# Two waits of a VectorE sum change places: the load on the sum, the earlier sum in a nop in front

## The chip, the cores and the metric

One core of a Trainium2 chip runs the kernel. The metric is device time in microseconds (us) of one execution; "the span" is the profiled execution from its first to its last instruction, 1.78 us shorter (160.52 of 162.30 us before).

## The reference

```python
x = random (32, 512, 1024) float32;  multiplier = 0.5
return (np.sum(x, axis=-1) * multiplier).astype(np.float32)
```

16,384 row sums over 67.11 MB of input; the output is 64 KB.

## The kernel before

Each of 128 partitions holds 128 rows, loaded 16 at a time. VectorE sums most blocks with one reduction. The last block comes in pieces, and its last row in two, cut at column 576, so that little work is left once the last bytes have landed.

```python
def nop_after(engine, waits_for, follows):
    i = engine.nop()
    for w in waits_for:
        tc.add_manual_dep(i.ins, w.ins.name, SYNC, reason="end seen here")
    for f in follows:
        tc.add_manual_dep(i.ins, f.ins.name, ORDER, reason="in this order")
    return i

def dve_span(t, r, lo, hi, dst, start=0.0):
    mid = (lo + hi) // 2
    return nc.vector.tensor_tensor_reduce(     # adds the two halves, then all of it to start
        out=t[:, r, lo:mid], in0=t[:, r, lo:mid], in1=t[:, r, mid:hi],
        scale=mul, scalar=start, op0=ADD, op1=ADD, accum_out=dst)
# ... all blocks but the last ...
cut = 576
# ... loads of rows 0-7, 8-12, 13-14 of the last block ...
for lo, hi in ((0, cut), (cut, D)):
    loads.append(nc.sync.dma_start(out=t[:, B - 1, lo:hi], in_=x_last[:, B - 1, lo:hi]))
# ... the other rows of the block, on VectorE and ScalarE ...
dve_span(t, B - 1, 0, cut, part)
final = dve_span(t, B - 1, cut, D, res[:, rows - 1 : rows], start=part)
# ... SyncE waits for everything and stores the last 16 columns ...
```

## Time and profile before

| | before |
|---|---|
| time, median of 3 | 162.13 us (162.12 to 162.49) |
| span | 160.5 us |
| last load lands | 157.72 us |
| last sum starts | 157.85 us |
| from the last landing to the end of the span | 2.80 us |

The table is read from the bottom. Up to 157.72 the loads run, and their queue is busy for 97.5% of the span; the last 2.80 us run one after the other: the last sum, its store, the closing barrier. Only the first 0.13 us of that, between landing and sum, is touched here.

### The profile page before, as it was taken

To read this page: it belongs to the slowest core of one execution; us is meant where nothing else is said; L and a number is where in the kernel's file an instruction comes from. 1 tells how busy PE (TensorE), PEld (TensorE's weight loads), DVE (VectorE), ACT (ScalarE), POOL (GpSimd) and SP (SyncE) were. 2 spreads that over 40 slices of the span, in tenths; PEclk is the share of its full clock that TensorE was granted. 3 is DMA by queue.
4 is the path that set the end of the run, shared out by engine and by line. 5 is a ranking of instruction groups with operands and counts; after the bars stand their busy time and mean duration, and the time that the engine had idled before them with its cause. 6 is when DMAs were issued, how large, how long until landed. Compare 5 with 4: busy or idle time off the path is not lost.

```text
span 160.5 us, 138 instructions
## 1 busy us (share of the span) xinstructions
DVE 119.3 (74%) x34; ACT 17.3 (11%) x31; POOL 0.2 (0%) x4
## 2 busy tenths in 40 slices
DVE  0000059998699968999599995999959999597443
ACT  0000000000000000000000000000000000599952
POOL 0000000000000000000000000000000000000000
DMA  8996996996996996996996997997998998999991
GB/s 261 523 523 261 523 506 278 523 490 294 523 490 294 523 490 294 523 490 294 523 490 294 523 474 310 523 441 343 523 425 359 523 425 359 392 433 425 439 368 50
DMA packets 2016, 67.18 MB, mean 418 GB/s; under 512 B 480, under 2 KB 608, under 8 KB 736
## 3 DMA queue, kind: packets, MB, share of 16 engines
q1 hardware_dynamic: 2016, 67.18, 97.5%
HBM read 67.11 MB, written 0.07 MB: 418 GB/s over the span
## 4 chain that ended last, share of the span: by engine, by line
DMA 75%; DVE 22%; SPq 1%; issue 0%; DVEq 0%
DMA xb<-in_x_dram 75%; DVE sums L96 21%; SPq L114 1%; DVE xb L80 0%; SPq L120 0%; SPq L94 0%; DVE res L99 0%; DVEq L80 0%; DVEq L201 0%
## 5 line engine op out<-in xcount | busy, mean ns | idle before, releaser
L96 DVE TENSOR_REDUCE sums<-xb 128x16 f32<-128x16384 f32 (+1 forms) x7 | 112.0, 16001 | 33.6 <-DMA xb<-in_x_dram 33.6
L70 ACT ACT_TABLE_LOAD x1 | 1.3, 1283 | 138.2 <-DMA xb<-in_x_dram 138.2
L70 ACT ACTIVATE xb<-xb 128x1024 f32<-128x1024 f32 x15 | 15.7, 1045 | 2.1 <-DMA xb<-in_x_dram 2.1
L80 DVE CUSTOM_DVE_ANT_0 xb<-xb 128x512 f32<-128x512 f32 (+1 forms) x9 | 5.6, 663 | 5.0 <-DMA xb<-in_x_dram 5.0
L70 ACT ACTIVATION_READ_ACCUMULATOR xb<-xb 128x1 f32 x15 | 2.8, 187 | 0.0
L99 DVE TENSOR_SCALAR res<-sums 128x16 f32<-128x16 f32 (+1 forms) x7 | 1.2, 174 | 0.2
L80 DVE DVE_READ_ACCUMULATOR2_ANT res<- 128x1 f32 x9 | 0.7, 83 | 0.0
L80 DVE CUSTOM_DVE_ANT_0 xb<-xb,part 128x224 f32<-128x224 f32 x1 | 0.5, 452 | 0.2 <-DMA xb<-in_x_dram 0.2
L187 POOL MEMSET const-bfloat16-1.0<- 128x1 bf16 x1 | 0.1, 102 | 0.0
L187 POOL MEMSET const-uint8-127<- 128x1 uint8 x1 | 0.1, 102 | 0.0
L187 POOL MEMSET const-float32-0.0<- 128x1 f32 x1 | 0.1, 99 | 0.2 <-issue 0.2
L187 POOL MEMSET const-float32-1.0<- 128x1 f32 x1 | 0.1, 99 | 0.0
L80 DVE DVE_READ_ACCUMULATOR2_ANT part<- 128x1 f32 x1 | 0.1, 83 | 0.0
## 6 DMA issues: line engine op xcount, KB each, us to landing
xb<-in_x_dram SPq DMA_DIRECT2D x1, 4096.0 KB, 31.1
xb<-in_x_dram SPq DMA_DIRECT2D x1, 2560.0 KB, 36.9
xb<-in_x_dram SPq DMA_DIRECT2D x1, 1024.0 KB, 38.9
xb<-in_x_dram SPq DMA_DIRECT2D x1, 288.0 KB, 39.1
xb<-in_x_dram SPq DMA_DIRECT2D x1, 224.0 KB, 39.2
xb<-in_x_dram SPq DMA_DIRECT2D x7, 40.8
out_dram<-res SPq DMA_DIRECT2D x1, 56.0 KB, 10.0
out_dram<-res SPq DMA_DIRECT2D x1, 8.0 KB, 1.4
```

Of the source, the lines that this page charges most:

```text
L70: acts.append(nc.scalar.activation(out=t[:, r, :], in_=t[:, r, :], func=mybir.ActivationFunctionType.Copy, scale=mul, accum_out=res[:, col ...
L80: return nc.vector.tensor_tensor_reduce(out=t[:, r, lo:mid], in0=t[:, r, lo:mid], in1=t[:, r, mid:hi], scale=mul, scalar=start, op0=ADD, o ...
L96: nc.vector.reduce_sum(out=sums[:, c0 : c0 + h], in_=t[:, 0:h, :], axis=mybir.AxisListType.X)
L99: nc.vector.tensor_single_scalar(out=res[:, c0 : c0 + h], in_=sums[:, c0 : c0 + h], scalar=mul, op=mybir.AluOpType.mult,)
L114: nc.sync.dma_start(out=t[:, lo:hi, :], in_=x_last[:, lo:hi, :])
L187: nc = _bacc.Bacc("TRN2", target_bir_lowering=False, num_devices=1)
```

## The change

The last sum needs two things: the last load, and part, the sum over the row's first 576 columns. The intent is to let it wait for the load alone, the later of the two, and to have the wait for part over and done with ahead of it.

```diff
-    dve_span(t, B - 1, 0, cut, part)
+    first = dve_span(t, B - 1, 0, cut, part)
+    part_seen = nop_after(nc.vector, [first], [])
     final = dve_span(t, B - 1, cut, D, res[:, rows - 1 : rows], start=part)
+
+    tc.add_manual_dep(final.ins, part_seen.ins.name, ORDER, reason="in this order")
+    tc.declare_no_dep(final.ins, first.ins.name, reason="waited for by the nop in front")
```

The diff seems to add an instruction; the prediction shows from the built programs that it does not, since an event-semaphore instruction (here one that only waits for semaphores; 21 ns on VectorE's sequencer in the trace before) already stood in front of the sum. Below, **old form** means load in front and part on the sum; **new form** means part in front and load on the sum.

## The prediction

Cut out of the recorded text below, and marked there, are a paragraph and a sentence on how the sequencer works, which no run here shows; that the wait for part has to stay somewhere was argued in them alone and is not shown either. Part's arm comes to -46 + 28 + 21 + 91 = +94 ns and the load's to 0 + 24 = +24, all from the trace before. "In that place" means the event-semaphore instruction in front of the sum, which loses the wait for the load.

> **What bounds the kernel now.** I read the page first, then the chain that ended last, then the instructions in order of time over the last microsecond, then the row view of the line that forms the sums, and last the trace's own semaphore records.
>
> The page gives the scale of things:
>
> ```profile
> span 160.5 us, 138 instructions
> DVE 119.3 (74%) x34; ACT 17.3 (11%) x31; POOL 0.2 (0%) x4
> q1 hardware_dynamic: 2016, 67.18, 97.5%
> DMA 75%; DVE 22%; SPq 1%; issue 0%; DVEq 0%
> ```
>
> The one DMA queue fills 97.5% of the 16 engines' time, and the loads carry three quarters of the chain. VectorE is busy 74% of the span and nothing near full. So the kernel is bound by reading 67.11 MB, and no arithmetic ahead of the last load can shorten it. The change touches only what follows that load. This is the end of the chain, with start, length and owner of each piece:
>
> ```profile
> 118.50 39.21 DMA xb<-in_x_dram
> 157.72 0.03 issue
> 157.74 0.02 DVEq L80
> 157.76 0.09 issue
> 157.85 0.45 DVE xb L80
> 158.31 0.01 DVEq L201
> ```
>
> The last load lands at 157.72. The last sum, which needs nothing else from memory, starts only at 157.85. Of that gap, a piece of 0.02 us is work of VectorE's sequencer (DVEq), with 0.03 before it and 0.09 after. Compare a place where the sum waits for its load itself, earlier in the same chain:
>
> ```profile
> 58.63 40.79 DMA xb<-in_x_dram
> 99.42 0.02 issue
> 99.44 17.23 DVE sums L96
> ```
>
> There the sum starts 0.02 us after the landing. So the last sum loses about 0.11 us (0.13 - 0.02) against an instruction that waits for its load itself. The row view of the summing line names the piece between, and the timeline gives the neighbours:
>
> ```profile
> L80 DVEq EVENT_SEMAPHORE  x1: 21/21/21, 157.7 to 157.7; - x1
> ```
>
> ```profile
> 157.19 0.46 DVE L80 CUSTOM_DVE_ANT_0 xb<-xb 128x288 f32<-128x288 f32 x1
> 157.41 0.19 ACT L70 ACTIVATION_READ_ACCUMULATOR xb<-xb 128x1 f32 x1
> 157.57 0.08 DVE L80 DVE_READ_ACCUMULATOR2_ANT part<- 128x1 f32 x1
> 157.85 0.45 DVE L80 CUSTOM_DVE_ANT_0 xb<-xb,part 128x224 f32<-128x224 f32 x1 [0.20 <-DMA xb<-in_x_dram]
> 158.23 0.08 DVE L80 DVE_READ_ACCUMULATOR2_ANT res<- 128x1 f32 x1
> 158.34 0.34 SPq L138 DMA_DIRECT2D out_dram<-res  x1
> ```
>
> The reader is to see that the value the last sum starts from (part) is finished at 157.57 + 0.08 = 157.65, only some 0.06 us ahead of the landing, and that the store follows the last sum directly.
>
> **What the built programs add.** The diff seems to add an instruction, but it doesn't. In the kernel before, the builder has already split the last sum's two waits: an event-semaphore instruction waits for the last load, and the sum itself waits for part. In the changed kernel the nop is that event-semaphore instruction: it waits for part, and the sum itself waits for the last load. Order, count and operands on every engine are the same, and SyncE's waits ahead of the store are unchanged. The change is a swap of two waits between two instructions.
>
> [...]
>
> **The change, step by step.** The semaphore records of the trace give finer times than the views; counted from the landing of the last load (157.715) they are, in ns:
> - part's accumulator read ends at -58; its semaphore update is recorded at -46.
> - the last load's sixteenth update is at 0.
> - the event-semaphore instruction starts at +28 and ends at +49.
> - the last sum starts at +140, so 91 ns after the event-semaphore instruction ended.
>
> The four sums that wait for a load in the instruction itself in the tail (of 512, 512, 512 and 288 elements) start 23, 23, 24 and 24 ns after the sixteenth update of their load.
>
> [...] Added: the wait for part in that place. I take the same costs for it: 28 ns until it passes, 21 ns of its own, 91 ns until the sum can start, 140 ns in all. It now starts from part's update at -46, so the sum is ready at -46 + 140 = +94. The other arm is the load, seen by the waiting sum at 0 + 24 = +24. The later arm decides: +94. Before it was +140. **The gain is 46 ns**, not the 116 ns (140 - 24) that the difference between the two forms suggests. With 140 ns of overhead on either arm, the gain is simply how much earlier part is ready than the last load: d = 46 ns in this trace, as long as d lies between -116 and +116.
>
> Beside other work or on the path? All of the last 0.14 us before the sum is on the path. After it: the last sum takes 452 ns, its result's update starts the store 17 ns later, and SyncE has passed its other waits (the last of them ends 211 ns after the landing, while the result comes at +612). So SyncE takes over the full 46 ns; even 116 would fit. The store's landing (1.4 us) and the closing barrier then move up as a block. Span 160.52 - 0.05 = 160.47; time 162.13 - 0.046 = **162.08 us**, that is 0.03% less.
>
> **Rivals.**
> 1. *The wait for the load vanishes from the sequencer altogether*: the sum starts 24 ns after the landing, gain 116 ns, 162.01 us. For it: the four direct waits. Against it: the nop is passed only after part, and 140 ns from there is 70 ns later than +24. It would need the 91 ns between the event-semaphore instruction and the sum to be shorter when no load ends the wait.
> 2. *A wait takes the place of the one removed, and d turns negative*: in other executions the last load may land sooner after the piece ahead of it. Part's sum starts 24 ns after its own piece lands and has its update 503 ns after that landing; the last piece landed 549 ns after it. A gap of 500 ns or less would make the swap a loss of the same size: some 0.03 us, 162.16 us. For it: two of the sixteen updates of each piece come some 200 ns behind the fourteenth, so a small shift in DMA moves d. Against it: both pieces are sent and end in the same way, so their distance should hold to some tens of ns.
> 3. *The last load is hidden anyway or another engine ends the span*: ScalarE's last sum ends at 157.60, before the landing, and SyncE has 0.4 us of slack, so I see no engine that takes the end over. Result would be 162.13 us.
> 4. *The transfer times themselves move*: with the same issues in the same order I expect no shift from the change, but the three times of before spread from 162.12 to 162.49, eight times the gain.
>
> **Range and chances.** The mechanism spans 161.98 to 162.20 (rivals 1 and 2 with some room). The spread of single runs, 0.37 us with one of three above, and a chip whose loads run a little differently widen it: 161.85 to 162.35. A move of 2% is 3.2 us; nothing after the landing of the last load could give or take that, since the whole stretch from there to the end of the span is 160.52 - 157.72 = 2.80 us. Within 2%: 0.99.
>
> **What would show it right or wrong.** In the changed profile the chain should end with part's accumulator read, a DVEq piece of 21 ns that starts some 28 ns after part's update, and the last sum about 140 ns after that update, no longer tied to the load's landing. If the sum starts 0.02 us after the landing and well under 140 ns after part's update, rival 1 holds. If the landing comes before part's update, rival 2 holds. The last sum should keep its 0.45 us, and the stretch from its start to the end of the span (2.66 us) should stay. What would make the time wrong without touching the steps is a shift of the loads by tenths of a microsecond, visible as a last landing away from 157.72.

## More of the kernel before

The prediction shows the lines; one more pair is wanted later, the start of the chain of waits (start, length, what):

```profile
0.43 40.93 DMA xb<-in_x_dram
41.36 0.02 issue
```

The first load of that chain lands at 41.36.

## The result, and the profile after

| | before | after |
|---|---|---|
| time, median of 6 | 162.12 us (162.11 to 162.49) | 162.10 us (161.99 to 162.25) |
| span, profiled run | 160.5 us | 160.2 us |

The ratio is 0.9995, with a 95% interval of 0.9982 to 1.0008. Ratios here are the mean time of one kernel's fast runs over that of the other's in the same rounds, so not quite the ratio of the medians. In time, the change can't be told from nothing. The predicted gain of 0.046 us is smaller than the scatter of either kernel, so the profile has to decide.

The head of the page after the change, its total busy time, its DMA queue and the chain's shares:

```profile
span 160.2 us, 138 instructions
DVE 119.3 (74%) x34; ACT 17.3 (11%) x31; POOL 0.2 (0%) x4
q1 hardware_dynamic: 2016, 67.18, 97.4%
DMA 75%; DVE 22%; SPq 1%; issue 0%; DVEq 0%
```

Same work, same instruction counts. The end of the chain of waits after the change:

```profile
118.24 39.23 DMA xb<-in_x_dram
157.47 0.08 issue
157.55 0.45 DVE xb L80
158.00 0.01 DVEq L205
```

(L205 is the new number of the line that was L201, since the diff adds four lines.) The three pieces between landing and sum (0.03, 0.02 and 0.09 us before) are now one of 0.08. The sequencer's piece hasn't vanished; it has moved in front of the landing, where the chain doesn't see it. The row view of the nop's line shows it, and the timeline shows the sums around it:

```profile
L59 DVEq EVENT_SEMAPHORE  x1: 21/21/21, 157.4 to 157.4; - x1
```

```profile
156.93 0.46 DVE L80 CUSTOM_DVE_ANT_0 xb<-xb 128x288 f32<-128x288 f32 x1
...
157.32 0.08 DVE L80 DVE_READ_ACCUMULATOR2_ANT part<- 128x1 f32 x1
157.55 0.45 DVE L80 CUSTOM_DVE_ANT_0 xb<-xb,part 128x224 f32<-128x224 f32 x1 [0.15 <-DMA xb<-in_x_dram]
```

The 0.08 us left after the landing are what remains of the way from the nop to the sum.

**A trap in these two profiles.** The span fell by 0.31 us, six times what was predicted, and most of it has nothing to do with the change. The start of the chain after the change:

```profile
0.43 40.66 DMA xb<-in_x_dram
41.09 0.02 issue
```

The first load landed 0.27 us earlier (41.36 - 41.09), more than 100 us before the changed instructions run, and the last landing is 0.25 us earlier (157.72 - 157.47). The first landing goes with neither form in the other runs: at the cut of 448 used further down it came at 41.18 in the old form and 41.30 in the new, at 704 at 41.03 in both. Only the remaining 0.06 us lie after the landing. Two spans whose loads are 0.27 us apart from the first landing on can't be compared for a change of 0.05 us. So all that follows is counted **from the landing of the last load** of the same execution, in ns, from the trace's semaphore records. There d is the time from part's semaphore update to that landing; it is negative where part comes later.

### The profile page after: what moved, and what is told of

Read it like the earlier page. It is cut to its first block, busy times and chain, and to the rows that moved or that the text cites. A ratio compares the mean times of both kernels' runs of the same rounds, so it can differ in the third digit from the quotient of the medians.

```text
span 160.2 us, 138 instructions
## 1 busy us (share of the span) xinstructions
DVE 119.3 (74%) x34; ACT 17.3 (11%) x31; POOL 0.2 (0%) x4
## 2 busy tenths in 40 slices
DMA packets 2016, 67.18 MB, mean 419 GB/s; under 512 B 480, under 2 KB 608, under 8 KB 736
## 3 DMA queue, kind: packets, MB, share of 16 engines
q1 hardware_dynamic: 2016, 67.18, 97.4%
## 4 chain that ended last, share of the span: by engine, by line
DMA 75%; DVE 22%; SPq 1%; issue 0%; DVEq 0%
DMA xb<-in_x_dram 75%; DVE sums L96 22%; SPq L114 1%; DVE xb L80 0%; SPq L120 0%; SPq L94 0%; DVE res L99 0%; DVEq L205 0%
```

## The experiments

The theory: whatever the instruction in front waits for costs 140 ns until the sum starts; whatever the sum itself waits for costs 24 ns; the later of the two arms decides. Written out, the sum starts at max(140, 24 - d) after the landing in the old form and at max(24, 140 - d) in the new. The main rival is that the new form is simply worth some 50 ns. The two agree at d = 46 and differ elsewhere. Moving the cut moves d, so both forms were run at other cuts. What was expected there of the sum's length, and of d at 704, agrees with estimates from the page before: a sum takes 689 ns at 512 elements and 459 at 288, so 1.03 ns more per element; 128 columns are 65.5 KB, 157 ns at the page's mean of 418 GB/s. At 704 that gives d = 46 - 66 - 157 = -177. This table holds all profiles; "rule" is the formula with that run's own d.

| run | form | cut | d | sum starts after landing | rule | the sum takes | store lands after landing |
|---|---|---|---|---|---|---|---|
| before | old | 576 | 46 | 140 | 140 | 452 | 2050 |
| before2 | old | 576 | 39 | 141 | 140 | 451 | 2050 |
| after | new | 576 | 56 | 84 | 84 | 450 | 1991 |
| a2 | new | 576 | 40 | 101 | 100 | 450 | 2016 |
| b448 | old | 448 | 271 | 140 | 140 | 517 | 2111 |
| a448 | new | 448 | 231 | 23 | 24 | 519 | 2005 |
| b656 | old | 656 | -67 | 139 | 140 | 410 | 2009 |
| b704 | old | 704 | -172 | 196 | 196 | 385 | 2038 |
| a704 | new | 704 | -171 | 311 | 311 | 387 | 2158 |
| a528 | new | 528 | 137 | 24 | 24 | 477 | 1955 |
| front | both waits in front | 576 | 44 | 126 | - | 453 | 2041 |
| prewait | new, a further wait in front | 576 | 48 | 78 | 92 | 452 | 1990 |
| prewait544 | the same | 544 | 96 | 31 | 44 | 469 | 1957 |

**Both forms once more (a2, before2).** Edit: none.

> The changed kernel once more, unchanged: a second profile and more times. Own theory: the sum again starts 140 ns after part's update, whatever the distance of that update from the landing; d should lie at 56 give or take some 20 ns, so the store lands some 1.99 us after the last load (2.05 before). In the time at most 0.05 us, too little to tell from the scatter of 0.1.

> The kernel before once more, for a second profile. Own theory: the sum starts 140 ns after the landing again, whatever d (40 to 60), and the store lands 2.05 us after the last load.

Measured: the sum started 141 ns after part's update in a2 (140 in the first profile after the change), and 141 ns after the landing in before2 (140). d was 39 to 56 in the four profiles at this cut. The mean start after the landing is 140.5 old and 92.5 new: a gain of 48 ns. In a2 the store landed 2.02 us after the load and not 1.99 as expected: of these 25 ns, 17 are the later start of the sum (101 against 84, since d was 40 and not 56), 7 are the store's own way from issue to landing (1428 against 1421), and 1 lies between. The time of a2 was 162.10 us (161.94 to 162.25) against 162.21 (162.09 to 162.39) of before on the same chip, ratio 0.9994 with an interval of 0.9982 to 1.0007: again not resolved.

The chain of a2 differs from that of the first profile after the change, and is worth a look:

```profile
157.00 0.46 DVE xb L80
157.46 0.02 DVE part L80
157.48 0.03 issue
157.51 0.02 DVEq L59
157.53 0.09 issue
157.62 0.45 DVE xb L80
```

This is the form that the prediction described: part's sum, part's read, the nop, the sum. In the first profile the chain led from the load instead. The timing rule is the same; the nop there ended 8 ns before the landing, in a2 it ended 9 ns after it, and the chain follows whatever was released last. A chain names one predecessor even where two are some ns apart.

**Part ready much earlier (b448, a448).** Edit, in each of the two forms:

```diff
-    cut = 576
+    cut = 448
```

> The kernel before with the last row cut at 448 of 1024 columns, so that the last load is longer and the sum ahead of it (part) is ready earlier. d is the time from part's semaphore update to the landing of the last load: 46 ns before, here some 240 by estimate (last piece 128 columns or 65 KB longer, VectorE not free for part before about 157.07). Own theory (an instruction in front costs 140 ns after whatever it waits for, a wait on the sum itself 24): the last sum starts 140 ns after the landing, as before. Rival A (the form is worth a fixed 50 ns) says the same here. The last sum takes 0.52 us (288 elements instead of 224).

> The changed kernel with the cut at 448, d some 240 ns. Own theory: part's arm (-240 + 140 = -100) is over before the landing, so the load's arm decides and the sum starts 24 ns after the landing; the gain against the same cut in the old form saturates at 116 ns. Rival A (a fixed gain of some 50 ns): the sum starts some 85 to 95 ns after the landing. Rival B (the changed form always starts 140 ns after part and never earlier than the load allows by another 90): about 115 after the landing.

The ends of the chain, old form first, then new:

```profile
157.55 0.03 issue
157.58 0.02 DVEq L80
157.60 0.09 issue
157.69 0.52 DVE xb L80
```

```profile
118.43 39.24 DMA xb<-in_x_dram
157.68 0.02 issue
157.70 0.52 DVE xb L80
```

140 ns against 23: the gain is 117, not 50. In the new form the nop ended 183 ns before the landing. A fixed gain (rival A) and a fixed remainder after the landing (rival B) both fall. In time, 162.22 us (162.19 to 162.29, 4 runs) against 162.11 (161.94 to 162.22, 4 runs) on one chip: the medians differ by about what the profiles say, but the ranges touch.

**Part ready after the load (b704, a704).** Edit, in each of the two forms:

```diff
-    cut = 576
+    cut = 704
```

> The kernel before with the cut at 704, so that the last load is short and part is ready only after it: d about -177 ns by estimate. Own theory: the wait in front passes early, the sum waits for part itself and starts about 24 ns after part's update, 200 ns after the landing. Rival A: 140 ns or more after the later of the two, that is over 300 after the landing.

> The changed kernel with the cut at 704, d about -177 ns. Own theory: the wait for part stands in front and now ends last, so the sum starts 140 ns after part's update, some 317 ns after the landing: the change turns into a loss of 116 ns. Rival A (a fixed gain of some 50 ns): the change still gains, so the sum starts earlier after part's update than in the old form with this cut.

The old form, where the sum itself waits for part, then the new, where the nop does:

```profile
157.43 0.03 issue
157.46 0.09 DVE part L80
157.55 0.02 issue
157.58 0.39 DVE xb L80
```

```profile
157.68 0.02 DVE part L80
157.70 0.03 issue
157.73 0.02 DVEq L59
157.75 0.09 issue
157.84 0.39 DVE xb L80
```

The two chains have changed roles: now the new form shows the 0.03, 0.02 and 0.09 us, and the old one shows 0.02. The sum starts 24 ns after part's update in the old form (196 after the landing, so the "over 300" of rival A falls) and 140 ns after it in the new. The same edit that gained 48 ns at a cut of 576 loses 115 here (311 - 196). It also shows that the cost doesn't come from waiting for a DMA rather than for VectorE's own semaphore: each of the two gives 140 in front and 24 on the sum. The times were 162.06 us (161.95 to 162.11) old and 162.26 (162.22 to 162.32) new, four runs each on one chip, and the ranges don't touch. The difference of 0.20 is more than the 0.115 of the mechanism. The two profiles differ in their last landing too, by about 0.15 us of the 0.27 between their spans, so part of the 0.20 is probably load scatter; that part is not explained further.

**Both waits in front (front).** The sum's own wait is set to a ScalarE row that ended long before. Why it keeps a wait of its own is shown by no run.

```diff
-    part_seen = nop_after(nc.vector, [first], [])
+    part_seen = nop_after(nc.vector, [first, loads[-1]], [])
...
+    tc.declare_no_dep(final.ins, loads[-1].ins.name, reason="waited for by the nop in front")
+    tc.add_manual_dep(final.ins, acts[-3].ins.name, SYNC, reason="ended long before")
```

> The changed kernel with both waits, for part and for the last load, in the instruction in front; the sum itself waits only for a ScalarE row that ended long before. Own theory [...]: the sum starts 140 to 155 ns after the landing, as in the kernel before, and the gain is gone. Rival (the gain came from the sum no longer waiting on VectorE's own semaphore): the sum starts well under 100 ns after the landing.

The sum started 126 ns after the landing. The rival (well under 100, because the wait for part is off the sum) falls, but the expectation of 140 to 155 was missed too, by 14 ns. The nop's row and the end of the chain:

```profile
L59 DVEq EVENT_SEMAPHORE  x1: 51/51/51, 157.5 to 157.5; - x1
```

```profile
118.30 39.22 DMA xb<-in_x_dram
157.52 0.03 DVEq L59
157.56 0.09 issue
157.65 0.45 DVE xb L80
```

The instruction's record is 51 ns long and not 21, and it begins 17 ns before the landing, 27 after part's update. So the record begins with the first wait and contains the second. It ended 34 ns after the landing (-17 + 51), where an instruction that waits for the load alone ended at 49 (28 + 21). The way from there to the sum was 92 ns, as before, so the whole difference lies ahead of its end.

**A further wait in front on purpose (prewait, prewait544).** If an instruction that has begun by an earlier wait passes its last one sooner, then giving the nop a wait that is long over, ahead of the wait for part, should save the same 14 ns.

```diff
     part_seen = nop_after(nc.vector, [first], [])
+    again = nop_after(nc.vector, [acts[-3]], [part_seen])
...
+    tc.add_manual_dep(final.ins, again.ins.name, ORDER, reason="in this order")
```

The builder joins the two nops into one event-semaphore instruction that waits for ScalarE first and for part second. In prewait544 the cut is 544 too.

> The changed kernel with a second wait in the instruction in front, for a ScalarE row that ended more than 3 us earlier, ahead of the wait for part. From the run with both waits in front, where that instruction had begun by its first wait and the sum started 126 ns after its second: the sum should start about 126 ns after part's update, 14 earlier than with one wait. Rival (each further wait in front only adds sequencer time): 147 to 155 ns after part's update.

> The same with the cut at 544: d some 108 by interpolation between 48 at 576 and 137 at 528. If the further wait takes 14 ns off, part's arm ends at 126 - 108 = 18 ns after the landing, so the load's arm decides: the sum starts 24 ns after the landing and takes 0.47 us, and the store lands 1.95 us after the last load. If it adds time, the sum starts 40 to 50 ns after the landing.

The ScalarE row had ended some 2.6 us before part's update, not more than 3 as written ahead. The nop's row in prewait:

```profile
L59 DVEq EVENT_SEMAPHORE  x1: 499/499/499, 157.0 to 157.0; - x1
```

It began early and contains the whole wait for part. The sum started 126 ns after part's update (127 in prewait544), where the plain new form needs 140. So the rival (147 to 155, an estimate without a source) falls. In prewait544 the sum was expected 24 ns after the landing and started at 31: d was 96 there and not 108, so part's arm (127 - 96) still ended last. That the way is shorter with a second wait in the instruction was measured three times (with front). Whether the number of waits or the early begin makes it shorter was not separated, and why, inside the sequencer, is not shown by these records.

**The two forms at their best cuts (a528, b656).** In the new form a lower cut helps until d reaches 116, where both arms meet; in the old form a higher cut helps until -116.

```diff
-    cut = 576
+    cut = 528      # in the new form; 656 in the old form
```

> The changed kernel with the cut at 528, where both arms should meet: d some 125 by interpolation between 56 at 576 and about 231 at 448. Own theory: the sum starts 24 ns after the landing (at most 35 if d falls short of 116) and takes 0.475 us (248 elements), so the store lands some 1.96 us after the last load: about 0.03 less than the changed kernel and 0.09 less than before. In the time about 162.03. If the gain had been fixed, a lower cut would only lengthen the last sum and the store would land 0.025 us later than in the changed kernel.

> The kernel before with the cut at 656, where the old form should be at its best: d about -90, the sum starts 140 ns after the landing still, and takes 0.41 us (184 elements). The store should land 2.01 us after the last load, 0.04 less than before, so moving the cut alone would give about what the swap gives at 576. If the old form were slower than the new by a fixed amount at any cut, it would stay at 2.03 or more.

In the new form with 528 the sum started 24 ns after the landing and the store landed 1955 ns after it: 95 less than before and 36 less than the first profile after the change. The old form with 656 came to 2009, between the two profiles of the new form at 576 (1991 and 2016). So the new cut alone is worth about what the swap alone is worth, and the swap with its own cut is 54 ns ahead of it. In time nothing of this is resolved: a528 162.12 us (162.01 to 162.41), ratio 0.9999 with an interval of 0.9985 to 1.0012; b656 162.11 (161.92 to 162.15), ratio 0.9993 with 0.9981 to 1.0006. The 162.03 expected of a528 was not seen. By the profile a528 has the shortest tail of all runs, with prewait544 (1957) beside it; by the clock it can't be called a better kernel.

## Why the prediction was right

- *What bounds the kernel.* Right: the last landing comes 2.80 us before the end, the queue is busy for 97.5% of the span, and busy times and instruction counts are the same after the change. What moved ahead of the last landing moved from the first load on, long before the changed instructions.
- *A swap and not an addition.* Right: 138 instructions in both, one event-semaphore instruction of 21 ns on VectorE's sequencer in front of the sum in both.
- *140 ns in front, 24 ns on the sum.* Right over all runs with a single wait in front: 139 to 141 and 22 to 24, with either kind of producer behind either kind of wait. No record shows what the last 91 to 92 ns of the 140 consist of.
- *The gain is d, not 116.* This was the step that mattered. It was right in the first profile (d 56, sum at 84, so 56 earlier than at 140), the mean over two profiles of each form is 48, and both the cap (117 at cut 448) and the change of sign (-115 at cut 704) were found where the rule puts them.
- *d = 46.* Right as a size: 39 to 56 in four profiles. It differs from execution to execution, so the predicted +94 was met by 84 and 101.
- *Nothing downstream eats the gain.* Right: the store began 486 ns after the sum's start (489 before) and landed 1421 ns after its issue in both.
- *The rivals.* Rival 1 falls: the way from part's update to the sum stayed 140 to 141. The sum does start 23 to 24 ns after the landing at 448 and 528, but because d is over 116 there, not because the way is shorter. Rival 2 (d negative) didn't occur at 576. Its size was put wrongly: with part's update 503 ns after its own piece, a gap of 500 between the two pieces would lose 3 ns; its 0.03 us would need a gap of some 473, and the four profiles had 541 to 559. The pair of late updates that it named came 207 and 216 ns behind the fourteenth of the last load before, but 29 and 67 after. Rival 4 was the one to beware of: loads that landed 0.25 us earlier made the fall of the span (306 ns) five times what lies after the landing (58 ns).
- *What the profile would show.* Half right. The first profile's chain led from the load, not from part's read and the nop; the described chain appeared in the second. The prediction didn't allow for the sum being within some ns of either release.
- *The time.* 162.08 predicted, 162.10 measured. That they lie so close is luck and doesn't confirm the 0.046 us: means of six runs differ by 0.085 (162.197 - 162.112), and the interval of the ratio contains 1. What the forecast's range allows for another chip was an estimate; the medians of before were 162.11 us on chip 8 and 162.21 on chip 12.

## What to carry to other kernels

When an instruction has two waits, put the one that ends last on the instruction itself and the earlier one in front; here the same edit gained 48 ns with the order right and lost 115 with it wrong. The most to be gained is the difference of the two ways (116 ns here), and the actual gain is the distance between the two events, so move the earlier event forward until that distance is covered, and no further where that lengthens what comes last: at 448 (d 231) the last sum took 519 ns and the store landed 2005 ns after the load, at 528 (d 137) 477 and 1955. For a gain below the scatter of the loads, count from the last landing within one trace, and distrust the span (here it fell by 306 ns, of which 58 lay after the landing).

## What else the traces show

- Where a VectorE instruction itself has the wait that ends last, it started 22 to 24 ns after the semaphore update (18 such waits in each of the first two profiles). Where an event-semaphore instruction in front of the sum has the one wait that ends last, 27 to 28 ns pass until it starts, 21 are its own, and 91 to 92 follow until the sum starts: 139 to 141 in all.
- With two waits in one event-semaphore instruction, its record begins before the last of them is over: it is 499 ns long in prewait, 480 in prewait544 and 51 in front, where 21 is the length with one wait.
- A wait that is over before the last one, in the same instruction, came with a shorter way to the sum: 126 to 127 ns in place of 140.
- What the wait for part costs depends on where it stands: 24 ns from part's update to the sum with the wait on the sum (b704), 140 with the wait in front (a704).
- A sum of 224 elements took 387 to 388 ns with a constant start value (part's own sum at cut 448) and 450 to 453 with part as its start value. That the start value is the cause was not tested by itself.
